# The recurrent half of the output projection as one Strassen step, with weight sums made by adding transfers, and the end of the recurrent branch ahead of the attention

## The chip, the core and the metric

The kernel runs on one core of a Trainium2 chip. The core has five engines that run side by side and wait for one another by semaphores: TensorE (PE; matrix products, with its weight loads shown as PEld), VectorE (DVE), ScalarE (ACT), GpSimd (POOL) and SyncE (SP), which here only issues transfers. Sixteen DMA engines carry the transfers. Weights and activations lie in the on-chip memory SBUF; products arrive in the eight banks of the accumulator memory PSUM, from which VectorE or ScalarE must fetch them.

The metric is the device time of one execution in microseconds, as the median of several runs. A profiled execution gives the trace: when each instruction ran, and what it waited for.

## What is computed

One layer of an encoder: 512 tokens, width 1024, all in float32. The part around the change is this:

```python
y_rnn = (h_f + h_b).astype(x.dtype) * jax.nn.gelu(gate)
...
y_attn = dilated_attention(qh, kh, vh, rel_bias)
mix = jnp.concatenate([rms_norm(y_rnn, norm_rnn_g[l]), rms_norm(y_attn, norm_attn_g[l])], axis=-1)
x = x + mix @ w_out[l]
h = rms_norm(x, mlp_norm_g[l])
x = x + jnp.square(jax.nn.relu(h @ w_up[l])) @ w_down[l]
```

`h_f` and `h_b` are the forward and the backward scan of the recurrent branch (512 channels), `y_attn` comes from eight heads of 64 channels. `w_out` is 1024 x 1024; its upper 512 rows take the recurrent half, its lower 512 rows the attention half. Each half is a product of 512 x 512 by 512 x 1024.

## The kernel before

**Precision.** Each float32 operand is split into a high part, rounded to the fp32r format by a copy, and a low part, the difference. `mm3` (L311) makes a product from three fp32r matmuls: high by high, high by low, low by high. In the text below one *step* is one `mm3`. The high part of a weight block of 128 x 1024 is made by `conv_hi` on ScalarE (L247, tile `whi`), the low part by `conv_lo` on VectorE (L269, tile `wlo`). `remake` makes the low part in another way: two ScalarE copies of 512 columns with the sign turned (L257), onto which two transfers from GpSimd's queue add the raw weights (L259); `conv_lo` then costs VectorE nothing for that block.

**Weights.** All weight blocks form a list `chunks`. `emit_dma` (L226) loads the next plain block into one of three buffers `wraw`, on SP's queue; `conv_lo` calls it when a block's raw weights are done with. The blocks of the recurrent half are the chunks from `C_WO` on, those of the attention half the ones from `C_WA` on. The attention half already goes by one Strassen step, in its form with seven products, in the order `OSEQ`: 11, s2, s3, s4, 21, s1, 22. The sums of its weight blocks are made on VectorE (`sum1` to `sum3` and one more, L1055 to L1066), those of its activations by `o_sum`.

**Order.** PE, ACT, DVE and POOL run strictly in the order in which the Python code issues their instructions. SP does so inside the attention loop as well; outside of it a planner orders SP.

**The attention loop** runs over pairs of heads i = 0 to 4 and steps u = 0 to 3. `att_s` makes the logits of pair i for two u at once (tile `ps`), `att_e` adds the bias and takes the exponential (VectorE and ScalarE, tile `e`), `att_t` turns the exponentials of pair i-1 on TensorE (tile `pt`, fetched by ScalarE as `ett`), `att_c` turns a small strip of them on VectorE, and `att_av` multiplies with the values (tile `pav`, fetched by VectorE as `yp`). `att_z` and `att_zd` send the reciprocal denominators through DRAM. In between, `fill(n)` takes the next n thunks from the list `fillers` and so keeps TensorE busy: first 48 steps of the query and key products for pairs 1 to 3, then the steps of the recurrent half of the output projection. Six are taken ahead of the loop. The table `FILL` says how many of the four places in a step take one; where it says nothing, all four do. The table `plan` holds what else is done in a step: a key (i, u, place). Between the two parts of the list, in (2, 2), stands `load_x`: it places the residual x and four blocks of `w_out` in the buffers that the last query-key product sets free, and spreads the loads over the following steps (`more`, taken by `add_x` at the end of each step).

**The recurrent branch's end.** `rnn_end` adds the two scans and multiplies by the gate (L597, L598), `rnn_sq` squares on ScalarE (L609), `y_add` adds the squares up (L615), `rnn_cols` makes the norm's factor per token, `rc[0]`. These are in `plan`, spread over the loop. `y_hi` and `y_lo` (L621, L625) scale by the norm's weight and split.

**The recurrent half of the projection** is `wo_thunks` (L981): 4 token tiles by 4 channel blocks for each half of the columns, 32 steps in all, each 128 x 128 by 128 x 512. Each of the 8 outputs has a PSUM bank of its own, and `end` multiplies it by `rc[0]` and adds it to x on VectorE:

```python
def end(n, tt):
    stt(x1[tt, n], pw[n, tt], rc[0][:, tt:tt + 1], x1[tt, n], op0=OP.mult, op1=OP.add)
```

By `FILL`, 24 of the 32 steps go into the loop and 8 behind it. Then follows the attention half (`wo_m`, `wo_x`), and the feed-forward part, which takes the rest of the time.

## Time and profile before

| | |
|---|---|
| median of 3 runs | 525.16 us (524.88 to 525.16) |
| the profiled execution's own time | 525.49 us |
| its span, first to last instruction | 523.7 us |
| granted TensorE clock, mean | 0.999 |
| HBM read | 95.59 MB, 191 GB/s over the span |
| steps of the recurrent half on TensorE | 139.6 to 179.6 us, among the attention's |
| `end` on VectorE (L986) | 8 times, 144.6 to 188.7 us |
| loads of x on SP (L1049) | 8 times, 139.9 to 152.6 us |

Times within the trace count from the span's first instruction. Matmuls are pipelined: a row's length (0.39 us for 512 columns) overlaps the next one's, and what counts is the distance from start to start, which the chain of waits gives as a matmul's share (0.23 us). For VectorE and ScalarE, too, the distance between the starts of neighbours that don't wait is what one instruction takes from its engine. A bracket at the end of a row gives the time that the engine stood idle ahead of it and what ended that.

### The profile page before, as it was taken

The numbers are of one execution on the slowest core, as the hardware profiler recorded it, in microseconds if no ns is written. First come the engines' busy times: TensorE is split into PE (matmuls) and PEld (weight loads), VectorE is DVE, ScalarE is ACT, GpSimd is POOL, SyncE is SP. The second block draws the span as 40 slices with busy tenths as digits, with TensorE's granted clock in tenths as the row PEclk, the third lists the DMA queues.
The fourth block names the chain that finished last, engine by engine and source line by source line (L and its number), as shares of the span: only waits on it lengthen the run. The fifth ranks groups of instructions, "written<-read, shape, count | busy, mean of one in ns | idle before, by whom it ended". The sixth has DMA issues, their size and how long they took to land.

```text
span 523.7 us, 8216 instructions
## 1 busy us (share of the span) xinstructions
PE 517.1 (99%) x3021; PEld 444.3 (85%) x3021; DVE 430.4 (82%) x668; ACT 352.2 (67%) x570; POOL 65.3 (12%) x89
## 2 busy tenths in 40 slices
PE   9999999999999999999999999999999999999995
PEld 8867888778777788899999888889999999888884
DVE  6899986788886898898789987789766978986885
ACT  7579946667857857586578666565667577655655
POOL 0173000000000321001300312001100300131000
PEclk9999999999999999999999999999999999999999
DMA  7636555266796499947595899976986497799704
GB/s 288 208 99 196 161 160 180 83 191 199 190 294 197 115 196 247 353 134 195 139 223 143 213 273 281 306 271 161 300 256 168 117 224 210 157 289 257 195 1 161
DMA packets 40329, 105.15 MB, mean 201 GB/s; under 512 B 5056, under 2 KB 13376, under 8 KB 40288
## 3 DMA queue, kind: packets, MB, share of 16 engines
q1 hardware_dynamic: 32448, 78.10, 44.5%
q0 software_dynamic: 7696, 26.32, 27.3%
q8 instruction: 24, 0.39, 0.3%
q10 hardware_dynamic: 144, 0.20, 0.1%
q14 instruction: 17, 0.14, 0.1%
HBM read 95.59 MB, written 4.29 MB: 191 GB/s over the span
## 4 chain that ended last, share of the span: by engine, by line
PE 99%; DVE 0%; issue 0%; DVEq 0%; ACT 0%; ACTq 0%
PE pu L314 10%; PE pu L312 10%; PE pu L313 10%; PE pd L314 10%; PE pd L312 10%; PE pd L313 10%; PE pqk L312 3%; PE pqk L314 3%; PE pqk L313 3%; PE pwo L312 3%; PE pwo L314 3%; PE pwo L313 3%; PE pav L942 2%; PE pt L842 2%; PE ps L806 2%; PE pp L312 1%
## 5 line engine op out<-in xcount | busy, mean ns | idle before, releaser
L269 DVE TENSOR_TENSOR wlo<-wraw,whi 128x1024 fp32r<-128x1024 f32 x71 | 86.6, 1220 | 24.0 <-ACT whi L247 23.9
L247 ACT ACTIVATE whi<-wraw 128x1024 fp32r<-128x1024 f32 x67 | 70.8, 1057 | 37.4 <-PE pd L314 18.4
L313 PE MATMUL pd<-wlo,ah 128*128 128x512 f32 (+1 forms) x195 | 75.2, 386 | 0.0
L312 PE MATMUL pd<-whi,ah 128*128 128x512 f32 (+1 forms) x195 | 75.2, 386 | 0.0
L314 PE MATMUL pd<-whi,al 128*128 128x512 f32 (+1 forms) x195 | 75.2, 386 | 0.0
L313 PE MATMUL pu<-hl,whi 128*128 128x256 f32 x224 | 63.4, 283 | 0.0
L314 PE MATMUL pu<-hh,wlo 128*128 128x256 f32 x224 | 63.4, 283 | 0.0
L312 PE MATMUL pu<-hh,whi 128*128 128x256 f32 x224 | 63.4, 283 | 0.0
L312 PE MATMUL pu<-h2h,whi 128*128 128x256 f32 (+1 forms) x200 | 60.1, 300 | 0.0
L313 PE MATMUL pu<-h2l,whi 128*128 128x256 f32 (+1 forms) x200 | 60.0, 300 | 0.0
L314 PE MATMUL pu<-h2h,wlo 128*128 128x256 f32 (+1 forms) x200 | 60.0, 300 | 0.0
L269 DVE TENSOR_TENSOR wlo<-tw,whi 128x1024 fp32r<-128x1024 f32 x37 | 45.2, 1221 | 17.7 <-ACT whi L247 17.7
L247 ACT ACTIVATE whi<-tw 128x1024 fp32r<-128x1024 f32 x38 | 40.1, 1058 | 24.9 <-PE pd L314 6.3
L312 PEld LDWEIGHTS pu<-hh,whi 128*128 128x128 f32 x224 | 43.0, 192 | 0.0
L313 PEld LDWEIGHTS pu<-hl,whi 128*128 128x128 f32 x224 | 43.0, 192 | 0.0
L314 PEld LDWEIGHTS pu<-hh,wlo 128*128 128x128 f32 x224 | 43.0, 192 | 0.0
L313 PEld LDWEIGHTS pd<-wlo,ah 128*128 128x128 f32 x195 | 36.6, 188 | 7.4
L312 PEld LDWEIGHTS pd<-whi,ah 128*128 128x128 f32 x195 | 36.6, 188 | 7.3
L314 PEld LDWEIGHTS pd<-whi,al 128*128 128x128 f32 x195 | 36.6, 188 | 7.4
L247 ACT ACTIVATE whi<-ts 128x1024 fp32r<-128x1024 f32 x24 | 25.4, 1060 | 25.2 <-PE pd L314 16.4
L313 PEld LDWEIGHTS pu<-h2l,whi 128*128 128x128 f32 x200 | 38.3, 191 | 1.3
L314 PEld LDWEIGHTS pu<-h2h,wlo 128*128 128x128 f32 x200 | 38.3, 191 | 1.3
(280 smaller groups left out, 1220.1 us busy)
## 6 DMA issues: line engine op xcount, KB each, us to landing
wraw<-in_w_up_dram SPq DMA_DIRECT2D x25, 512.0 KB, 4.8
ts<-in_w_dn_dram POOLq DMA_DIRECT2D x24, 512.0 KB, 13.5
wraw<-in_w_dn_dram SPq DMA_DIRECT2D x24, 512.0 KB, 8.7
tw<-in_w_up_dram SPq DMA_DIRECT2D x15, 512.0 KB, 6.7
tw<-in_w_up_dram POOLq DMA_DIRECT2D x15, 512.0 KB, 7.5
wraw<-in_w_in_dram SPq DMA_DIRECT2D x13, 512.0 KB, 4.3
ts<-in_w_dn_dram SPq DMA_DIRECT2D x8, 512.0 KB, 9.0
tw<-in_w_dn_dram SPq DMA_DIRECT2D x8, 512.0 KB, 7.0
```

The lines of the kernel that those rows point to most:

```text
L247: act(hi, raws[i], AF.Copy)
L269: nc.vector.tensor_tensor(lo, r, f(splits[i][0]), op=OP.subtract)
L312: nc.tensor.matmul(o, lhsT=a[0], rhs=b[0], start=bool(first), stop=False, skip_group_check=on)
L313: nc.tensor.matmul(o, lhsT=a[0], rhs=b[1], start=False, stop=False, skip_group_check=on)
L314: nc.tensor.matmul(o, lhsT=a[1], rhs=b[0], start=False, stop=bool(last), skip_group_check=on)
L806: nc.tensor.matmul(psq[p, u][e][:, :NK], lhsT=qs_[p, a][r, P * qt:P * qt + P], rhs=kks[p][r, b, w:w + NK], start=i == 0, stop=i == 2)
L842: nc.tensor.transpose(pt[:, i * P:(i + 1) * P], en[h][qt][:, k:k + P], ident)
L942: nc.tensor.matmul(pav[p][a, co], lhsT=vs[:, jt, h * DH:(h + 1) * DH], rhs=et[h, jt][:, ci], start=jt == 0 and i == 0, stop=jt == 3 and i ...
```

## The change

The recurrent half goes by the same Strassen step as the attention half. `wo_thunks` runs over seven products in the order `RSEQ`: 11, s2, s3, s4, s1, 22, 21, with 2 token tiles and 2 channel blocks each, 28 steps in all. Products 11, s2, s3 and s4 add up in one pair of PSUM banks, s1 and 22 in a second pair, 21 has a third. After each product's token tile, `end` adds the partial sum so far to the quarter of x that `OEND` names; there are 14 of them instead of 8.

- The sums of weight blocks s1, s2 and s3 are loads on SP followed by adding transfers on GpSimd's queue into the same `wraw` buffer; s4 is made by another adding transfer into the buffer of s2, once that one's low part is made. The recurrent half has 7 chunks instead of 4, and `C_WA` and `C_UP` move by 3.
- The sums of activations are made by `strassen_rows`, the attention half's functions turned into a closure that serves both. `rnn_at` scales the branch's output by the norm's weight in place. `rnn_neg` makes the negated factor.
- `rnn_end`, the squares and three of their sums move from the attention loop to the first query-key product and the six steps ahead of the loop; the three sums become adding transfers on GpSimd's queue.
- In `load_x`, the pieces of x come ahead of blocks 22 and 21 and of the sums, which move to later steps; the blocks 21, s2, s3 and s4 of the attention half get their low parts by `remake` within the steps (4, 0) to (4, 2). Before, s4 and 21 did so behind the loop, and s2 and s3 had a `conv_lo`.
- `FILL` takes 20 steps into the loop and leaves 8 behind it.

```diff
+RSEQ = ("11", "s2", "s3", "s4", "s1", "22", "21")
+RSUM = {"s1": ("12", "11"), "s2": ("12", "11", "22"), "s3": ("12", "22")}
...
-    C_G, C_V, C_QK, C_WO, C_WA, C_UP = 4, 8, 12, 20, 24, 31
+    C_G, C_V, C_QK, C_WO, C_WA, C_UP = 4, 8, 12, 20, 27, 34
...
             r = stream.tile([P, 1024], FT, name="wraw", tag="wraw", bufs=3)
-            nc.sync.dma_start(r, source(chunks[i]))
+            c = chunks[i]
+            if isinstance(c, tuple) and c[0] == "r":
+                b = RSUM.get(c[1], (c[1],))
+                nc.sync.dma_start(r, rblock(b[0]))
+                for n in b[1:]:
+                    nc.gpsimd.dma_start(r, rblock(n), accum_op=OP.add)
+            else:
+                nc.sync.dma_start(r, source(c))
             raws[i] = r
...
             if isinstance(c, tuple) and c[0] == "o":
                 return
+            if isinstance(c, tuple) and c[0] == "r":
+                if c[1] == "s2":
+                    nc.gpsimd.dma_start(r, rblock("21"), accum_op=OP.add)
+                    raws[C_WO + RSEQ.index("s4")] = r
+                elif c[1] not in ("22", "21"):
+                    emit_dma()
+                return
...
-        if half in ssy:
+        if half in ssy and half == 0:
+            nc.gpsimd.dma_start(ssy[0], q, accum_op=OP.add)
+        elif half in ssy:
             nc.vector.tensor_tensor(ssy[half], ssy[half], q, op=OP.add)
...
+    o_hi, o_lo, o_hi2, o_lo2, o_sum, o_part = strassen_rows(at)
+    r_hi, r_lo, r_hi2, r_lo2, r_sum, r_part = strassen_rows(yrnn)
+    OEND = {"11": (0, 0), "21": (0, 0), "s1": (1, 1), "22": (0, 1), "s2": (0, 1), "s3": (1, 1), "s4": (1, 0)}
...
-        order = [(0, tt, k) for tt in range(4) for k in range(4)] + [(1, tt, k) for h in (0, 2) for tt in range(4) for k in (h, h + 1)]
+        order = [(w, tt, k) for w in RSEQ for tt in range(2) for k in range(2)]
...
+        def end(j):
+            w, tt, _ = order[2 * j]
+            i, n = OEND[w]
+            g = 2 * i + tt
+            stt(x1[g, n], pw[j], (nrc0 if n else rc[0])[:, g:g + 1], x1[g, n], op0=OP.mult, op1=OP.add)
+
+        def mk(b, w, tt, k):
             def run():
+                j = b // 2
+                new = w in ("11", "s1", "21")
                 if k == 0:
+                    pw[j] = ps_("pwo", "pj") if new else pw[j - 2]
+                hi, lo = splits[C_WO + b // 4]
+                sl = slice(k * S, (k + 1) * S)
+                mm3(pw[j], r_part(w, tt, k), (hi[:, sl], lo[:, sl]), k == 0 and new, k == 1, True)
+                if b % 4 == 1:
+                    conv_hi(C_WO + b // 4 + 3)
+                if b % 4 == 3:
+                    conv_lo(C_WO + b // 4 + 3)
+                if k == 0 and 0 < j < 12:
+                    end(j - 1)
             return run
...
+    RNN = {8: ((rnn_end, 0),), 10: ((rnn_end, 1), (rnn_sq, 0)), 11: ((rnn_end, 2), (rnn_sq, 1)), 13: ((rnn_sq, 2),)}
...
-        more.append([w_in(b22, "22")])
-        more.append([sum1, x_in(2, 0), x_in(3, 0), w_in(b21, "21")])
-        more.append([sum2, x_in(0, 1)])
-        more.append([sum3, x_in(1, 1)])
-        more.append([x_in(2, 1), x_in(3, 1)])
-        more.append([emit_dma])
-        more.append([emit_dma])
-        more.append([emit_dma])
+        more.append([x_in(0, 1), x_in(1, 1)])
+        more.append([w_in(b22, "22"), x_in(2, 1), x_in(3, 1)])
+        more.append([w_in(b21, "21"), x_in(2, 0), x_in(3, 0)])
+        more.append([sum1])
+        more.append([sum2])
+        more.append([sum3, remade_o("21"), remade_o("s2")])
+        more.append([remade_o("s3"), emit_dma])
+        more.append([remade_o("s4"), emit_dma])
...
+    plan = {(0, 0, 0): [op(rnn_at, 2), op(r_sum, "s1", 0)], (0, 0, 2): [op(rnn_at, 1), op(r_sum, "s2", 0)], (0, 0, 3): [op(rnn_at, 3), op(r_sum, "s3", 0)],
+            (0, 1, 1): [op(r_sum, "s1", 1)], (0, 2, 3): [op(r_sum, "22", 0)],
+            (1, 0, 2): [op(r_sum, "s2", 1)], (1, 1, 0): [op(r_sum, "s3", 1)], (1, 1, 2): [op(r_sum, "22", 1)],
+            (1, 3, 2): [op(r_hi, "11", 0), op(r_hi, "11", 1)], (2, 0, 0): [op(r_lo, "11", 0), op(r_lo, "11", 1)], (2, 0, 2): [rnn_cols],
+            (2, 0, 4): [op(r_hi2, "s2")], (2, 1, 2): [rnn_neg], (2, 1, 4): [op(r_lo2, "s2")], (2, 2, 3): [op(r_hi2, "s3")], (2, 3, 1): [op(r_lo2, "s3")],
+            (3, 0, 1): [op(r_hi2, 0)], (3, 0, 3): [op(r_lo2, 0)], (3, 1, 1): [op(r_hi2, 1)], (3, 1, 3): [op(r_lo2, 1)],
+            (3, 2, 1): [op(r_hi2, "s1")], (3, 2, 3): [op(r_lo2, "s1")], (3, 3, 1): [op(r_hi2, "22")], (4, 0, 1): [op(r_lo2, "22")]}
...
+        if n == 2:
+            rnn_end(3)
+            add()
+            rnn_sq(3)
+            rnn_at(0)
+            add()
+        if n == 4:
+            add()
+            add()
         fill(1)
...
-    FILL = {(3, 0): (1, 1, 1, 0), (3, 1): (1, 1, 1, 0), (3, 2): (1, 1, 1, 0), (4, 0): (0, 1, 0, 0), (4, 1): (0, 1, 0, 1), (4, 2): (0, 1, 0, 0), (4, 3): (0, 1, 0, 0)}
+    FILL = {(3, 0): (1, 1, 1, 0), (3, 1): (1, 1, 0, 0), (3, 2): (1, 1, 0, 0), (3, 3): (1, 1, 1, 0), (4, 0): (0, 1, 0, 0), (4, 1): (0, 1, 0, 0), (4, 2): (0, 1, 0, 0), (4, 3): (0, 1, 0, 0)}
...
+    emit_dma()
     fill(1)
-    conv_lo(C_WA + 2)
     att_av(3, range(4))
...
-    remake(C_WA + OSEQ.index("s4"))
     fill(1)
     att_y(3)
     yss = col_sums(ssy[1])
     fill(4)
-    remake(C_WA + OSEQ.index("21"))
+    st["wo"](11)
     fill(len(fillers))
```

The steps, their `end` and their place by `FILL` are then: b0, b1 in (2, 2); b2 to b5 in (2, 3); b6 to b8 in (3, 0); b9, b10 in (3, 1); b11, b12 in (3, 2); b13 to b15 in (3, 3); b16 to b19 in (4, 0) to (4, 3), one each; b20 to b27 behind the loop. `end(j)` belongs to the two steps b = 2j and 2j + 1 and is issued with step 2j + 2. `conv_lo` of the blocks s4, s1, 22, 21 and of the attention half's 11 is issued with steps b3, b7, b11, b15 and b19.

## The prediction

> **What bounds the kernel now.** I read the busy shares first, then the chain of waits.

> ```profile
> PE 517.1 (99%) x3021; PEld 444.3 (85%) x3021; DVE 430.4 (82%) x668; ACT 352.2 (67%) x570; POOL 65.3 (12%) x89
> PE 99%; DVE 0%; issue 0%; DVEq 0%; ACT 0%; ACTq 0%
> ```

> TensorE is busy all the time and the chain runs through it for 99% of the span. So a matmul taken out is worth its pitch, and a hole made in TensorE's work costs its full length: nothing later waits for anybody else and could give it back. What must be asked is whether the other engines still keep ahead where the change adds to their work. The stages of the old projection, by the view of windows (us; busy PE, PEld, DVE, ACT, POOL; granted clock, DMA share):

> ```profile
> 95.00:139.30 44.30, 44.30 (x259) 34.58 (x256) 37.67 (x100) 32.35 (x75) 1.04 (x1) 1.00 0.59 163
> 139.30:159.10 19.80, 19.80 (x115) 16.00 (x115) 15.26 (x42) 14.19 (x39) 0.00 (x0) 1.00 0.92 282
> ```

> From 139 to 159 VectorE has 15.3 of 19.8 us taken, and the DMA engines are at 0.92. The work that the change adds falls mostly there.

> **The change: TensorE.** One step (b of the list `order`) is three matmuls. 32 steps become 28, so 12 matmuls go. The chain (start, length) holds exactly twelve between these two rows:

> ```profile
> 141.77 0.23 PE pwo L312
> ...
> 143.15 0.23 PE pwo L312
> ...
> 144.50 1.33 PE ps L806 x12
> ...
> 159.09 0.66 PE pt L842 x6
> 159.74 5.76 PE pav L942 x48
> 165.50 0.43 PE pwo L312
> ```

> 144.50 - 141.77 = **2.73 us removed**. Three of the four steps go ahead of the `pav` at 159.74, so with full cover it would start at 157.69.

> **A new order between TensorE and VectorE.** Before, each output tile had its own PSUM bank and `end` read it when it liked. Now the products 11, s2, s3 and s4 add up in the same two banks, and `end` reads each partial sum in between: step b4 must wait for `end(0)`, b6 for `end(1)`, up to b14, then b20 and b22. VectorE works in the written order, so everything ahead of an `end` now holds TensorE. VectorE's timeline gives the durations as distances from start to start:

> ```profile
> 140.38 0.74 DVE L625 SCALAR_TENSOR_TENSOR yl<-gt,vt,yh 128x512 fp32r<-128x512 f32 x1
> ...
> 142.28 0.65 DVE L784 TENSOR_TENSOR kk<-kraw,kk 128x512 fp32r<-128x512 f32 x1
> 142.85 1.22 DVE L269 TENSOR_TENSOR wlo<-wraw,whi 128x1024 fp32r<-128x1024 f32 x1
> 144.59 0.75 DVE L986 SCALAR_TENSOR_TENSOR x<-pwo,rcol,x 128x512 f32<-128x512 f32 x1 [0.53 <-DMA x<-in_xn_dram]
> 145.67 0.59 DVE L822 CUSTOM_DVE_ANT_0 e<-ps,tw 128x416 f32<-128x416 f32 x1 [0.33 <-PE ps L806]
> ...
> 146.70 0.30 DVE L851 STREAM_TRANSPOSE ett<-e 128x32 f32<-128x32 f32 x2
> 146.93 0.31 DVE L871 RECIPROCAL rz<-zz 128x32 f32<-128x32 f32 x1
> ...
> 147.41 1.18 DVE L1055 TENSOR_TENSOR ws<-ws,wraw 128x1024 f32<-128x1024 f32 x1
> 148.51 0.58 DVE L822 CUSTOM_DVE_ANT_0 e<-ps,tw 128x416 f32<-128x416 f32 x1
> ...
> 149.75 0.71 DVE L986 SCALAR_TENSOR_TENSOR x<-pwo,rcol,x 128x512 f32<-128x512 f32 x1
> 150.38 1.21 DVE L1059 TENSOR_TENSOR tw<-ws 128x1024 f32<-128x1024 f32 x1
> ...
> 159.11 1.23 DVE L269 TENSOR_TENSOR wlo<-wraw,whi 128x1024 fp32r<-128x1024 f32 x1 [2.16 <-ACT whi L247]
> 160.26 0.74 DVE L986 SCALAR_TENSOR_TENSOR x<-pwo,rcol,x 128x512 f32<-128x512 f32 x1
> ```

> So the softmax part of one attention step (two e and the small transposes) is 1.26, its two e alone 1.03; the reciprocal part 0.48; a sum of 1024 columns 1.10; an `end` 0.63; a low half of 512 columns 0.57 (142.28 to 142.85); one of 1024 columns, `conv_lo`, 1.15.

> VectorE in the new order, by attention step (i, u), from 140.38, where the `yl` that stood there is gone:
> - (2,3): 1.26 + key low half 0.57 + `end(0)` 0.63 + s3 low 0.57 + `conv_lo` 1.15 + `end(1)` 0.63 = 4.81
> - (3,0): 1.26 + 0.48 + 0.63 + 1.15 + 0.63 + 0.57 = 4.72
> - (3,1): 1.26 + 0.63 + 0.57 = 2.46
> - (3,2): 1.26 + 1.15 + 0.63 + 0.57 + sum1 1.10 = 4.71

> That is 16.70 us, and 1.03 more for the two e of (3,3), for whose exponentials the transposes ahead of `pav` wait. TensorE needs less: from 141.11 (the transposes of 0.66 ahead of the first chain row) to 159.09 are 18.0 us for these four steps and (3,3); without the three b steps 15.9, and 13.2 without (3,3) itself (0.66 and three b of 0.68).

> **Waits inside it.** `end(0)` also adds x, which landed only at 144.59 (the bracket above), behind a store that the last query-key matmul sets free. Here it comes up at 142.21: 2.38 us. TensorE reaches b4 at 143.15 (third chain row), so b4 stands 144.59 + 0.75 - 143.15 = 2.2 us: this alone takes four fifths of the gain. How long the other pieces of x take:

> ```profile
> L1049 SPq DMA_DIRECT2D x<-in_xn_dram x8: 424/434/1492, 139.9 to 152.6; - x8
> DMA to landing us min/median/max: 4.1/5.1/5.6
> ```

> Two more pieces now stand on SP's queue behind a weight load whose buffer comes free only with a `conv_lo`. x(0,1) is behind block 21, which waits for the `conv_lo` of s4's weights, done at 146.94: issued at 147.37 (0.43 for the load's own issue), landed at 151.47 at the shortest; `end(2)` comes up at 149.61 (after 0.30 for the logits that the late b4 delays) and waits 1.86. x(2,1) is behind the load after s1's `conv_lo` (153.25) and another: issued at 154.11, landed at 158.21; `end(4)` comes up at 155.71 and waits 2.50. The median landing would add 1.0 to each. In all 2.38 + 0.30 + 1.86 + 2.50 = 7.04, and 140.38 + 17.73 + 7.04 = 165.15 for the second e of (3,3).

> [...]

> ```profile
> 157.41 0.64 ACT L823 ACTIVATE e<-e,mn 128x416 f32<-128x416 f32 x1
> ...
> 166.82 0.87 ACT L845 ACTIVATE ett<-pt 128x384 f32<-128x384 f32 x2 [0.53 <-PE pt L842]
> ```

> One exponential (0.64) and the second head's half of the transposes (0.33) later `pav` starts: 165.15 + 0.97 = 166.1, 8.4 us after 157.69. **Front: 8.4 lost.**

> **Behind `pav`.** VectorE's rows there:

> ```profile
> 165.57 0.69 DVE L948 TENSOR_TENSOR yp<-pav,zrow 128x512 f32<-128x512 f32 x1 [2.14 <-PE pav L942]
> 166.18 0.68 DVE L615 TENSOR_TENSOR ysq<-ysq 128x512 f32<-128x512 f32 x1
> ...
> 168.34 0.42 DVE L919 TENSOR_TENSOR osum<-at 128x256 f32<-128x256 f32 x1 [0.15 <-ACT at L962]
> ...
> 170.15 0.29 DVE L851 STREAM_TRANSPOSE ett<-e 128x32 f32<-128x32 f32 x2
> ```

> After the second y, which waits for both `pav` groups (5.76 + 0.1), stand ahead of `end(8)`: y 0.61, low half 0.57, `end(7)` 0.63, 0.60, sum3 1.10, 0.22, the sums 1.81 (168.34 to 170.15), the sum for s4 1.10, 0.22, and `end(8)` 0.63: 7.5, done 13.4 after the start of `pav`. TensorE wants b20 after 5.76 + 0.90 + 3 x 1.35 = 10.7 (0.90: a step whose first matmul takes 0.43; 1.35: transposes and a step). 2.7 lost, and 0.3 at the third `pav`, whose small transposes come later too. ScalarE has `remake` for four blocks in these steps: four of its 512-column copies, at 0.6 each by the exponential's row, go ahead of the evacuation (`ett`) of (4,1), where 0.53 was spare. That could cost 2.4 - 0.5 = 1.9 more, or nothing, since VectorE holds b20 anyway. I take nothing: VectorE's sum rests on rows of this very place. **Back: 3.0 lost.**

> **Edits that I put at nothing, and their bounds.** The recurrent ends move ahead of the attention:

> ```profile
> 90.28 0.69 DVE L765 TENSOR_TENSOR kraw<-pqk,rrow 128x512 f32<-128x512 f32 x1 [1.36 <-PE pqk L314]
> 96.52 0.69 DVE L597 TENSOR_TENSOR ga<-ga,hs 128x512 f32<-128x512 f32 x1
> ...
> 97.85 0.68 DVE L761 SCALAR_TENSOR_TENSOR qraw<-pqk,rrow 128x512 f32<-128x512 f32 x1
> ```

> Three pairs of 1.33 (96.52 to 97.85) now stand ahead of `kraw`, which waited 1.36 here: at most 2.6 late. Between its product and the first logits TensorE has six steps, 6 x 0.68 = 4.1; `kraw`, ScalarE's copy and the low half take some 2.0 of it (0.69, 0.64 and 0.57 by the rows above). I take nothing; the bounds are 0 and 0.6. Weights by adding transfers:

> ```profile
> 93.88 9.10 SPq L230 DMA_DIRECT2D wraw<-in_w_out_dram  x2
> wraw<-in_w_out_dram SPq DMA_DIRECT2D x5, 512.0 KB, 3.4
> tw<-in_w_up_dram POOLq DMA_DIRECT2D x15, 512.0 KB, 7.5
> 121.47 1.05 ACT L247 ACTIVATE whi<-wraw 128x1024 fp32r<-128x1024 f32 x1
> ```

> s2's weights are one load and two additions; the load is the second of the first row, ended at 102.98 and begun some 0.4 before. 102.6 + 3.4 + 2 x 7.5 = 121.0, needed at 121.47. At a DMA share of 0.59 I take 7.5, so nothing; 3 us more for each would hold ScalarE, and TensorE with it, by up to 5.5. The squares' sums as three adding transfers on POOL end long before they are read. No gain below nothing is left in these: TensorE had no holes to close.

> **The sum.** -2.73 + 8.4 + 3.0 = +8.7 on the profiled execution's 525.49 us (span 523.7); the median of the runs is 0.33 lower, so 525.2 + 8.7 = **533.9 us**, 1.7% slower.

> **Rivals.**
> - *Full cover (faster).* If `end` always comes before its bank is wanted, only 2.73 are left: 522.4. Deciding point: the first `end` done by 143.15; against it stands the bracket at 144.59. Chance 0.10.
> - *Only x's first wait* (no difference): -2.73 + 2.2, 524.6. It needs VectorE to do 16.7 us of work in 13.2: chance 0.12.
> - *VectorE's work, but no waits on SP's queue*: 1.86 and 2.50 fall away: 165.15 - 4.36 = 160.79, `pav` at 161.8, 4.1 lost; -2.73 + 4.1 + 3.0 = +4.4, 529.6. For it: x can land while VectorE is late. Chance 0.25.
> - *The forecast*, 531 to 537: 0.38.
> - *More of the same*: median landings (2.0) and ScalarE's 1.9: 537.8. Chance 0.11.
> - *A falling clock*: holes could lower the granted clock, which is below 1.00 in the last stage alone:

> ```profile
> 441.00:523.70 82.70, 76.86 (x350) 63.88 (x348) 65.92 (x93) 49.76 (x79) 9.65 (x11) 0.99 0.69 183
> ```

> Eight steps at half speed would add 8 x 0.68 = 5.5: 539.4. My longest single hole is 2.5 us. Chance 0.04. [...]

> Within 0.2% (1.05 us) a run can't be told from no change. Faster 0.10, same 0.12, slower 0.78. The range, 524.4 to 538.5, leaves out full cover and the falling clock.

> **What would show it.** Right: TensorE idle at b4, at the second logits of pair 3 and ahead of `pav`, released by VectorE's evacuation; `end(0)`, `end(2)`, `end(4)` waiting for x; VectorE nearly full from 140 to 165; TensorE's busy time 2.7 to 4 us less, the span longer. Wrong: `pwo` at an even pitch with no holes, or x landed ahead of its `end`; or holes at 95 to 125, which would be the weights.

## The result, and the profile after

Median of the runs of the changed kernel: **548.74 us** (546.28 to 549.52), against 525.14 us (524.88 to 525.22) of the kernel before on the same chip: a ratio of 1.0444, 95% interval 1.0423 to 1.0465. The forecast was 533.9 us, with a range up to 538.5. The direction was right; the loss is nearly three times the one forecast and lies outside the range.

The profiled execution took 548.65 us, its span 546.8 us. The page gives busy shares, the clock granted to TensorE by slices (tenths), and the chain of waits:

```profile
PE 521.7 (95%) x3009; PEld 444.4 (81%) x3009; DVE 437.8 (80%) x685; ACT 360.5 (66%) x585; POOL 75.8 (14%) x101
PEclk9999999997979999999999999999999999999999
PE 80%; DVE 7%; DMA 6%; ACT 3%; issue 2%; SPq 0%; DVEq 0%; ACTq 0%
```

TensorE has its 12 instructions less (3009 for 3021), yet is busy 4.6 us longer: from 128.27 to 135.10 and from 152.17 to 159.00 us its granted clock was 0.50 (the windows below), and there matmuls of 512 columns started 0.43 us apart (131.74 to 134.73) instead of 0.23. The chain, which ran through TensorE alone before, now goes through VectorE, the DMA and ScalarE for 16% of the span. The timeline of TensorE, longer idle stretches (start, length, tile, idle time before and what ended it):

```profile
128.76 0.48 PE L864 MATMUL pt<-ident,e 128*128 128x128 f32 x1 [2.32 <-ACT ett L867]
129.76 1.33 PE L864 MATMUL pt<-ident,e 128*128 128x128 f32 x5 [0.53 <-ACT e L845]
...
145.48 0.40 PE L337 MATMUL pwo<-whi,oh 128*128 128x512 f32 x1
...
154.88 0.79 PE L337 MATMUL pwo<-whi,oh 128*128 128x512 f32 x1 [5.83 <-DVE x L1021]
...
169.94 0.50 PE L337 MATMUL pwo<-whi,oh 128*128 128x512 f32 x1 [1.76 <-DVE x L1021]
...
173.54 0.50 PE L337 MATMUL pwo<-whi,oh 128*128 128x512 f32 x1 [1.27 <-DVE x L1021]
...
176.55 1.06 PE L864 MATMUL pt<-ident,e 128*128 128x128 f32 x5 [1.25 <-ACT e L845]
177.55 5.83 PE L974 MATMUL pav<-ett,vs 128*64 128x416 f32 x48
...
187.03 0.93 PE L864 MATMUL pt<-ident,e 128*128 128x128 f32 x6 [1.40 <-ACT ett L867]
...
190.38 0.93 PE L864 MATMUL pt<-ident,e 128*128 128x128 f32 x6 [1.73 <-ACT ett L867]
```

Three rows divide the loss into the terms of the forecast: the first step of the projection (145.48), the value products of pairs 1 and 2 (177.55), and the first matmul of the feedforward (`pu`), which closes the stretch. The starts of these three in every kernel of this study, and the distances between them:

| kernel | median us | ratio to before [95%] | first step at | to `pav` | to `pu` |
|---|---|---|---|---|---|
| before | 525.14 | | 139.57 | 20.10 | 40.83 |
| changed, if nothing waited | | | 139.57 | 18.05 | 40.15 |
| changed | 548.74 | 1.0444 [1.0423, 1.0465] | 145.48 | 32.07 | 45.72 |
| e1_plain_s2 | 540.68 | 1.0299 [1.0280, 1.0317] | 140.32 | 30.49 | 45.75 |
| e2_x_first | 540.36 | 1.0287 [1.0268, 1.0305] | 145.82 | 22.95 | 45.75 |
| e3_early_end | 525.38 | 1.0003 [0.9993, 1.0012] | 139.56 | 20.11 | 40.82 |
| e4_remake_late | 549.57 | 1.0473 [1.0454, 1.0492] | 144.22 | 31.09 | 47.90 |
| e5_both | 534.29 | 1.0178 [1.0158, 1.0198] | 139.77 | 22.72 | 45.76 |
| e6_own_bank | 534.95 | 1.0187 [1.0170, 1.0203] | 140.52 | 24.08 | 45.77 |
| e7_early_s2 | 534.92 | 1.0198 [1.0171, 1.0226] | 140.23 | 23.24 | 45.76 |
| e8_early_splits | 535.61 | 1.0195 [1.0168, 1.0223] | 139.38 | 22.87 | 45.87 |
| e9_no_x | 534.51 | 1.0180 [1.0163, 1.0197] | 139.38 | 23.61 | 45.77 |
| e10_no_remake | 533.44 | 1.0157 [1.0140, 1.0174] | 140.40 | 22.73 | 43.94 |
| e11_sums_pool | 536.65 | 1.0214 [1.0187, 1.0240] | 140.44 | 22.46 | 49.25 |
| e13_splits_no_x | 532.00 | 1.0120 [1.0095, 1.0145] | 140.67 | 20.02 | 45.76 |
| e14_no_pool | 530.19 | 1.0094 [1.0075, 1.0113] | 140.29 | 20.33 | 43.79 |
| e12_all | 527.42 | 1.0043 [1.0028, 1.0058] | 140.04 | 19.23 | 42.86 |

The starts and distances are those of the one profiled execution of each kernel. The runs were made on several chips: the kernel before has a median of 525.38 us beside e1 to e4, 525.20 beside e5 to e8, 524.70 beside e9 to e12 and 525.67 beside e13 and e14, so medians of different groups can't be compared to better than about 1 us. One of the four runs of e14_no_pool was slow (1322.85 us) and is left out.

The second row is the one before less the matmuls removed: nine of the twelve lie ahead of `pav`, and 9 x 0.2275 = 2.05, 3 x 0.2275 = 0.68. Against it the changed kernel loses 145.48 - 139.57 = **5.9** ahead of the projection, 32.07 - 18.05 = **14.0** in front of `pav` and 45.72 - 40.15 = **5.6** behind it. Less 2.73 that is 22.8 of the 23.1 us by which the span grew. The forecast had 0, 8.4 and 3.0.

**The 5.9 ahead of the projection.** First SP's and GpSimd's issues of the recurrent weights, then the adding transfers' median time to landing from 88 to 130 (last figure), then ScalarE's copy of s2's weights:

```profile
95.88 8.63 SPq L244 DMA_DIRECT2D wraw<-in_w_out_dram  x2
```

```profile
108.17 0.86 POOL L246 DMA_DIRECT2D wraw<-in_w_out_dram  x1 [8.20 <-DMA tw<-nbd]
117.28 1.75 POOL L246 DMA_DIRECT2D wraw<-in_w_out_dram  x2 [8.25 <-DMA tw<-nbd]
```

```profile
wraw<-in_w_out_dram POOLq DMA_DIRECT2D x5, 512.0 KB, 9.9
```

```profile
127.27 1.06 ACT L265 ACTIVATE whi<-wraw 128x1024 fp32r<-128x1024 f32 x1 [5.57 <-DMA wraw<-in_w_out_dram]
128.24 0.85 ACT L867 ACTIVATE ett<-pt 128x384 f32<-128x384 f32 x2
```

s2's load is the second of the first row. The second addition waits for the first: issued at 108.17 and 117.28 (the other issue in that row is s3's), 9.1 apart, the second landed about 127.2. (The brackets name `tw<-nbd`, another transfer; in e7_early_s2 below the trace puts the same wait down to `wraw` itself.) So the copy of the weights, due at 121.47 before, came at 127.27, and in ScalarE's written order the softmax's evacuation `ett` stood behind it. That makes the holes of 2.32 and 0.53 us. The clock fell in the first of them, at 128.27. Windows of TensorE's timeline (stretch, length, busy PE and the other engines, then the granted clock, third from the end):

```profile
124.86:128.27 3.41, 1.58 (x14) 1.06 (x12) 0.00 (x0) 1.00 (x2) 0.00 (x0) 1.00 1.06 224
...
128.27:131.69 3.42, 2.40 (x8) 1.86 (x9) 1.75 (x3) 3.42 (x12) 0.86 (x1) 0.50 1.05 243
131.69:135.10 3.41, 3.41 (x9) 2.64 (x8) 1.68 (x8) 1.36 (x5) 0.00 (x0) 0.50 1.11 298
135.10:138.52 3.42, 3.42 (x19) 2.87 (x18) 3.18 (x11) 2.57 (x5) 0.01 (x1) 1.00 0.80 183
```

For 6.83 us the granted clock was 0.50; TensorE was busy 2.40 + 3.41 = 5.81 of it. Taken as half the work, that is an estimated 2.9 lost; by the two distances of 0.43 and 0.23 it is 2.7. 2.32 + 0.53 + 2.9 = 5.75, nearly all of the 5.9.

There was an earlier wait in this stage, on VectorE. Its first sum of activations waited 2.50 us for ScalarE, which scales the branch's output there (`rnn_at`), and a low half of weights stood behind that sum:

```profile
99.37 0.42 DVE L945 TENSOR_TENSOR osum<-gt 128x256 f32<-128x256 f32 x1 [2.50 <-ACT gt L1049]
...
102.94 1.22 DVE L287 TENSOR_TENSOR wlo<-wraw,whi 128x1024 fp32r<-128x1024 f32 x1
```

SP issued s2's load as that low half ended, at 104.2 where the kernel before has 102.6. It also cost TensorE something: the logits at 101.62 waited 0.43 for VectorE. The two traces don't run level up to here (VectorE's `qraw` starts at 84.84 before, at 84.13 here). Counted from that row, the stage loses 6.6, and the 0.9 beyond the 5.75 stands in e7_early_s2 too (140.23 - 84.64 = 55.59 against 139.57 - 84.84 = 54.73), but not in e3_early_end, which has no such sums.

**The 14.0 in front of `pav`.** SP's and VectorE's rows:

```profile
141.46 0.33 SPq L244 DMA_DIRECT2D wraw<-in_w_out_dram  x1
...
145.44 0.33 SPq L1096 DMA_DIRECT2D ws<-in_w_out_dram  x1
145.88 1.30 SPq L1093 DMA_DIRECT2D x<-in_xn_dram  x2
```

```profile
154.08 0.75 DVE L1021 SCALAR_TENSOR_TENSOR x<-pwo,rcol,x 128x512 f32<-128x512 f32 x1 [5.90 <-DMA x<-in_xn_dram]
...
169.13 0.75 DVE L1021 SCALAR_TENSOR_TENSOR x<-pwo,nrc,x 128x512 f32<-128x512 f32 x1 [3.50 <-DMA x<-in_xn_dram]
```

x(0,0) was issued at 145.88 behind two loads of 512 KB (141.46 and 145.44) and landed 8.2 us later; `end(0)` stood 5.90 us at the head of VectorE's queue and b4 5.83 us behind it. The clock was at 0.50 again, from 152.17 to 159.00:

```profile
148.76:152.17 3.41, 0.30 (x2) 0.00 (x0) 0.00 (x0) 2.69 (x7) 0.00 (x0) 1.00 0.99 329
...
152.17:155.58 3.41, 0.69 (x2) 0.60 (x3) 1.50 (x3) 0.00 (x0) 0.00 (x0) 0.50 0.19 64
155.58:159.00 3.42, 3.42 (x14) 2.42 (x14) 1.64 (x2) 0.00 (x0) 0.00 (x0) 0.50 0.37 110
159.00:162.40 3.40, 3.24 (x21) 2.31 (x18) 2.80 (x10) 2.17 (x7) 0.00 (x0) 1.00 0.96 280
```

0.69 + 3.42 = 4.11 busy at a clock of 0.50: 2.06 lost by the same estimate of half the work. b4's hole is 3.6 longer than the 2.2 forecast; 3.6 + 2.06 = 5.7 is as much as the difference between 14.0 and 8.4. That it fits so well is partly luck, since other waits of the forecast moved both ways: `end(2)` didn't wait for x (forecast 1.86), `end(4)` waited 3.50 (forecast 2.50).

**The 5.6 behind `pav`.** ScalarE's timeline ahead of the first late `ett`: the table load, four 512-column copies of `remake`, then the evacuation for which TensorE waits 1.40 us.

```profile
183.03 1.28 ACT L1200 ACT_TABLE_LOAD   x1
...
184.43 1.13 ACT L275 ACTIVATE wlo<-ws 128x512 fp32r<-128x512 f32 x2
185.47 1.13 ACT L275 ACTIVATE wlo<-tw 128x512 fp32r<-128x512 f32 x2
186.51 0.85 ACT L867 ACTIVATE ett<-pt 128x384 f32<-128x384 f32 x2
```

### The profile page after: what moved, and what is told of

It is laid out like the page before. It is cut to its first block, busy times and chain, and to the rows that moved or that the text cites. A ratio compares the mean times of both kernels' runs of the same rounds, so it can differ in the third digit from the quotient of the medians.

```text
span 546.8 us, 8272 instructions
## 1 busy us (share of the span) xinstructions
PE 521.7 (95%) x3009; PEld 444.4 (81%) x3009; DVE 437.8 (80%) x685; ACT 360.5 (66%) x585; POOL 75.8 (14%) x101
## 4 chain that ended last, share of the span: by engine, by line
PE 80%; DVE 7%; DMA 6%; ACT 3%; issue 2%; SPq 0%; DVEq 0%; ACTq 0%
PE pu L337 10%; PE pu L338 10%; PE pu L339 10%; PE pd L337 9%; PE pd L338 9%; PE pd L339 9%; DMA wraw<-in_w_out_dram 2%; PE pav L974 2%; PE pp L337 1%; PE pp L338 1%; PE pp L339 1%; PE pv L339 1%; PE pv L337 1%; PE pv L338 1%; DMA kk<-kk 1%
## 5 line engine op out<-in xcount | busy, mean ns | idle before, releaser
L287 DVE TENSOR_TENSOR wlo<-wraw,whi 128x1024 fp32r<-128x1024 f32 x74 | 90.1, 1218 | 24.5 <-ACT whi L265 24.2
L265 ACT ACTIVATE whi<-wraw 128x1024 fp32r<-128x1024 f32 x70 | 73.9, 1056 | 43.2 <-PE pd L339 18.2
L287 DVE TENSOR_TENSOR wlo<-tw,whi 128x1024 fp32r<-128x1024 f32 x36 | 44.0, 1222 | 19.8 <-ACT whi L265 19.8
L337 PEld LDWEIGHTS pu<-h2h,whi 128*128 128x128 f32 x200 | 38.3, 191 | 1.3
## 6 DMA issues: line engine op xcount, KB each, us to landing
wraw<-in_w_up_dram SPq DMA_DIRECT2D x25, 512.0 KB, 4.8
ts<-in_w_dn_dram POOLq DMA_DIRECT2D x24, 512.0 KB, 13.0
wraw<-in_w_dn_dram SPq DMA_DIRECT2D x24, 512.0 KB, 8.4
tw<-in_w_up_dram SPq DMA_DIRECT2D x15, 512.0 KB, 6.1
tw<-in_w_up_dram POOLq DMA_DIRECT2D x15, 512.0 KB, 8.5
wraw<-in_w_in_dram SPq DMA_DIRECT2D x13, 512.0 KB, 3.4
ts<-in_w_dn_dram SPq DMA_DIRECT2D x8, 512.0 KB, 7.4
tw<-in_w_dn_dram SPq DMA_DIRECT2D x8, 512.0 KB, 8.9
```

Of the source, the lines that this page charges most:

```text
L265: act(hi, raws[i], AF.Copy)
L287: nc.vector.tensor_tensor(lo, r, f(splits[i][0]), op=OP.subtract)
L337: nc.tensor.matmul(o, lhsT=a[0], rhs=b[0], start=bool(first), stop=False, skip_group_check=on)
```

## The experiments

### Late weights and x's place on the queue

Run e1_plain_s2:

```diff
-RSUM = {"s1": ("12", "11"), "s2": ("12", "11", "22"), "s3": ("12", "22")}
+RSUM = {"s1": ("12", "11"), "s2": ("12",), "s3": ("12", "22")}
```

> Leaves out the two adding transfers of s2's weights (block 12 alone is loaded), so the weights of s2 and s4 are not the sums. Theory: the late weights of s2 (5.57 us of ScalarE's wait, TensorE holes of 2.3 and 0.5 us behind it, and some 6 us at half clock) cost 4 to 8 us: 540 to 545 us, ScalarE's copy of s2's weights back at about 121.5, no hole before 138. Rival, that VectorE's work holds the evacuations from 145 on anyway: 547 or more, since TensorE then only waits longer there.

540.68 us, 8.1 less than the changed kernel. The copy of s2's weights is back in its place, without a wait, and TensorE has no hole from 103 to 140:

```profile
122.22 1.04 ACT L265 ACTIVATE whi<-wraw 128x1024 fp32r<-128x1024 f32 x1
```

The first step comes at 140.32 instead of 145.48. So the weights were nearly the whole of the first term; what is left is the wait at the activation sums, which this kernel still has.

Run e2_x_first: the loads of the recurrent blocks 22 and 21 and of the attention's blocks 11 and 12 go behind the first pieces of x.

```diff
-                elif c[1] not in ("22", "21"):
+                elif c[1] == "11":
...
-        w_in(b12, "12")()
         x_in(0, 0)()
-        more.append([x_in(1, 0)])
+        x_in(1, 0)()
         more.append([x_in(0, 1), x_in(1, 1)])
-        more.append([w_in(b22, "22"), x_in(2, 1), x_in(3, 1)])
-        more.append([w_in(b21, "21"), x_in(2, 0), x_in(3, 0)])
-        more.append([sum1])
+        more.append([emit_dma, w_in(b12, "12")])
+        more.append([x_in(2, 1), x_in(3, 1), emit_dma])
+        more.append([x_in(2, 0), x_in(3, 0), emit_dma, w_in(b22, "22")])
+        more.append([w_in(b21, "21"), sum1])
```

> The whole computation; SP issues x's pieces ahead of the loads of blocks 22 and 21 and of the first attention block, which are taken out of the low halves and put behind them. Theory (x(0,0), issued behind a load that waited for a low half, landed at 154.1 and held b4 for 5.8 us, x(2,1) held end(4) for 3.5): b4's hole falls to 3 us or less, 540 to 544 us. Rival, that VectorE's work from 145 to 178 sets pav's start whatever x does: the waits for x go, pav moves by 2 us at most, 546 or more.

540.36 us. x's first pieces are issued no earlier than before, and yet `end(0)` starts at 148.93, with no wait:

```profile
146.02 1.76 SPq L1093 DMA_DIRECT2D x<-in_xn_dram  x4
```

```profile
148.93 0.75 DVE L1021 SCALAR_TENSOR_TENSOR x<-pwo,rcol,x 128x512 f32<-128x512 f32 x1
```

So it was not the time of issue but the megabyte issued ahead of it: x landed in 2.9 us at most instead of 8.2. From the first step to `pav` 22.95 us instead of 32.07. The rival (VectorE sets `pav`'s start whatever x does) fell.

Run e5_both has both edits.

> Both edits of the first two runs together: s2's weights as one plain load (s2's and s4's weights are then not the sums) and x's pieces issued first. Theory: two separate losses of about 8 us each, so they add: 531 to 534 us, no hole before 145, and what is left above before is VectorE's work and ScalarE's evacuations behind pav. Rival, that they hide the same loss (TensorE late by the one is what the other waits for): 537 or more.

534.29 us. The two gains of 8.06 and 8.38 add but for 2.0 (548.74 - 534.29 = 14.45), so they are two losses, and the rival (one loss that both hide) fell. In no stage from 88 to 201 was the granted clock under 1.00.

Run e7_early_s2 keeps the whole computation: e2_x_first, and s2's load changes places with block 11's.

```diff
     plain = deque(i for i, c in enumerate(chunks) if in_order(c))
+    at20 = plain.index(C_WO)
+    plain[at20], plain[at20 + 1] = C_WO + 1, C_WO
```

> The whole computation; x's pieces first as before in this study, and s2's load ahead of block 11's, so that its two adding transfers start some 4 to 8 us earlier. Theory (the transfers are late by about as much as they start late): within 2 us of the run with both edits, 531 to 536 us, no hole at 128. Rival, that the adding transfers or the DMA queues are too slow however early they start: 538 or more, with ScalarE's copy of s2's weights still behind 125.

534.92 us. The additions are issued at 101.06 and 106.68 instead of 108.17 and 117.28, and ScalarE's copy of s2's weights waits for nothing. Started 7 us earlier, the additions are in time, the first of them in 5.6 us instead of 9.1. These two reorderings, which leave no work out, give back 13.8 of the 23.6 us.

### The ends ahead of the attention

Run e3_early_end is the kernel before with `rnn_end`, `rnn_sq` and the squares' adding transfers where the change has them, and no Strassen step:

```diff
-        if half in ssy:
+        if half in ssy and half == 0:
+            nc.gpsimd.dma_start(ssy[0], q, accum_op=OP.add)
+        elif half in ssy:
...
+    RNN = {8: ((rnn_end, 0),), 10: ((rnn_end, 1), (rnn_sq, 0)), 11: ((rnn_end, 2), (rnn_sq, 1)), 13: ((rnn_sq, 2),)}
...
+        for fn, t in RNN.get(n, ()):
+            fn(t)
...
+        if n == 2:
+            rnn_end(3)
+            add()
+            rnn_sq(3)
+            add()
```

> The kernel before, with only the recurrent ends moved ahead of the attention and the squares' sums made by adding transfers; no Strassen step. Theory: they cost nothing and, since VectorE's steps of the attention are then lighter, bring nothing either: 524.6 to 525.6 us. Rival, that their 4 us on VectorE at 90 to 98 and POOL's transfers are part of the loss: 526.5 or more, with holes in TensorE between 88 and 125.

525.38 us beside 525.38 for the kernel before: nothing, within 0.1%. The row sums of the change aren't in this kernel. TensorE has no hole from 88 to 139.3:

```profile
88.00:139.30 51.30, 51.30 (x291) 40.21 (x290) 38.83 (x100) 36.11 (x79) 3.70 (x4) 1.00 0.65 174
```

### Is it the shared buffer, VectorE's work, or x?

Run e6_own_bank stands on e5_both.

```diff
-                new = w in ("11", "s1", "21")
+                new = True
```

> As the run with both edits, and every block's sum gets a PSUM buffer of its own, so that no product waits for the evacuation of the product before it in a shared buffer; what a product would have added to the sum before it is left out. Theory: the holes at pwo are waits for a shared buffer that VectorE is late to read, and VectorE has more work there than TensorE leaves time for, so the holes move to the softmax's buffers and the time falls by 0 to 2 us. Rival, that the sharing itself (one step between an evacuation and the next use) is the loss: 3 us or more below the run with both edits.

534.95 us, no change. TensorE still waits for VectorE's evacuations, now twice ahead of `pav`, where e5_both has one such wait of over 0.3 us, 1.29 at 158.49:

```profile
156.75 0.50 PE L337 MATMUL pwo<-whi,oh 128*128 128x512 f32 x1 [1.53 <-DVE x L1021]
...
160.35 0.50 PE L337 MATMUL pwo<-whi,oh 128*128 128x512 f32 x1 [1.29 <-DVE x L1021]
```

A buffer of its own for each product doesn't help here, since the evacuations as such come late.

Runs e8_early_splits and e9_no_x each change e7_early_s2 in one thing: the splits of four blocks of rows move ahead, or x is left out.

```diff
-            (3, 0, 1): [op(r_hi2, 0)], (3, 0, 3): [op(r_lo2, 0)], (3, 1, 1): [op(r_hi2, 1)], (3, 1, 3): [op(r_lo2, 1)],
-            (3, 2, 1): [op(r_hi2, "s1")], (3, 2, 3): [op(r_lo2, "s1")], (3, 3, 1): [op(r_hi2, "22")], (4, 0, 1): [op(r_lo2, "22")]}
+            (0, 1, 3): [op(r_hi2, 0)], (0, 2, 1): [op(r_lo2, 0)], (0, 3, 1): [op(r_hi2, 1)], (0, 3, 3): [op(r_lo2, 1)],
+            (1, 0, 1): [op(r_hi2, "s1")], (1, 0, 3): [op(r_lo2, "s1")], (1, 2, 1): [op(r_hi2, "22")], (1, 2, 3): [op(r_lo2, "22")]}
```

> The whole computation; the run before, and the splits of rows 0, 1, s1 and 22 (four copies on ScalarE, four subtractions on VectorE of 0.6 us each) are moved from the stretch of 142 to 165 back to that of 100 to 135. Theory: VectorE's work inside 140 to 178 is what is left of the front's loss, 2.3 us of it go: 1.5 to 3.5 us below the run before. Rival, that what is left lies in the softmax's waits and behind pav: within 1 us of the run before.

```diff
-            stt(x1[g, n], pw[j], (nrc0 if n else rc[0])[:, g:g + 1], x1[g, n], op0=OP.mult, op1=OP.add)
+            stt(x1[g, n], pw[j], (nrc0 if n else rc[0])[:, g:g + 1], x1[g, n] if (g, n) in seen else ssy[0], op0=OP.mult, op1=OP.add)
+            seen.add((g, n))
...
-            return lambda: nc.sync.dma_start(x1[g, n], xn[2 * g + n])
+            return lambda: None
```

> As the run with s2's load first, and x left out: its eight transfers are not issued, and the first evacuation into each piece adds the row of squares in place of x, with the same instruction. Theory now (what is left of the front's loss is VectorE's in-order queue held at its head by x's landings, 1.1 and 1.8 us): 2 to 4 us below the run with s2's load first, no hole at b4. Rival (VectorE's sheer work in 140 to 163): within 1 us of it.

535.61 and 534.51 us: neither moved anything beyond 1 us, both theories missed. Once the splits are gone, VectorE waits for x in their place (e8_early_splits, VectorE's timeline):

```profile
143.32 0.75 DVE L1023 SCALAR_TENSOR_TENSOR x<-pwo,rcol,x 128x512 f32<-128x512 f32 x1 [1.13 <-DMA x<-in_xn_dram]
...
154.19 0.75 DVE L1023 SCALAR_TENSOR_TENSOR x<-pwo,nrc,x 128x512 f32<-128x512 f32 x1 [1.78 <-DMA x<-in_xn_dram]
```

Without x the splits stand there instead. If each covers the other, both edits together must give what neither gives alone. Run e13_splits_no_x has both:

> As the run with s2's load first, with both edits that alone changed nothing: the splits moved early and x left out. Theory (VectorE's work and x's landings cover each other): 2 to 4 us below that run, 531 to 533 us, with the value products of pairs 1 and 2 starting 2 to 4 us earlier. Rival (what helped in the run with everything was the sums on GpSimd or the copies left out): within 1 us of it, 534 or more.

532.00 us (530.46 to 532.50, where e7_early_s2 had 534.32 to 537.07): 2.9 less, and from the first step to `pav` 20.02 instead of 23.24. The wait ahead of the last transposes is 0.37 instead of 1.22:

```profile
159.69 1.06 PE L866 MATMUL pt<-ident,e 128*128 128x128 f32 x5 [0.37 <-ACT e L847]
```

### Behind the value products

Run e4_remake_late, on the changed kernel:

```diff
-        more.append([sum3, remade_o("21"), remade_o("s2")])
-        more.append([remade_o("s3"), emit_dma])
-        more.append([remade_o("s4"), emit_dma])
+        more.append([sum3])
+        more.append([emit_dma])
+        more.append([emit_dma])
...
+    remake(C_WA + OSEQ.index("s4"))
...
+    remake(C_WA + OSEQ.index("21"))
```

> The whole computation; the low halves of the attention blocks s2 and s3 go back to VectorE and those of s4 and 21 back behind the loop, as in the kernel before, so that ScalarE has four remakes less inside pair 4. Theory (ScalarE's remakes ahead of the evacuations ett make the holes of 1.40 and 1.73 us behind pav): 1 to 3 us less than the changed kernel, 545.5 to 547.5. Rival, that VectorE holds pair 4: no change or slower, 548 to 551, with the holes named for VectorE instead.

549.57 us, no gain. The hole ahead of `ett` shrinks, others grow, at VectorE's evacuation and then at ScalarE's splits of the attention's rows. Behind the last of them the clock was at 0.50 from 204.64 to 208.06, with TensorE busy all the time: by the estimate of half the work, 1.7 of the 2.2 us by which the last stretch is longer. TensorE's rows:

```profile
185.27 0.93 PE L864 MATMUL pt<-ident,e 128*128 128x128 f32 x6 [0.52 <-ACT ett L867]
188.92 0.50 PE L337 MATMUL pwo<-whi,oh 128*128 128x512 f32 x1 [2.02 <-DVE x L1021]
...
203.30 0.47 PE L337 MATMUL pwo<-whi,oh 128*128 128x512 f32 x1 [2.76 <-ACT oh L923]
```

This moves work from one engine to the other and can't price it. Run e10_no_remake, on e7_early_s2, leaves it out:

```diff
+            if isinstance(c, tuple) and c[0] == "o" and c[1] in ("21", "s2", "s3", "s4"):
+                splits[i] += (splits[i][0],)
+                return
...
-        return lambda: remake(C_WA + OSEQ.index(n))
+        return lambda: None
```

> As the run with s2's load first, and the low halves of the attention blocks 21, s2, s3 and s4 are left out (their first halves stand in), so ScalarE has eight 512-column copies less and nothing takes their place on VectorE. Theory (the copies ahead of the evacuations ett make the holes of 1.4 and 1.7 us behind pav): 2 to 3.5 us below that run. Rival (VectorE's sums and evacuations hold the last product there anyway): within 1 us of it, the holes named for VectorE.

533.44 us: 1.5 less, short of the 2 to 3.5 expected, and only 1.0 less where each is set against the kernel before on its own chip (8.7 above it, e7_early_s2 9.7). The median alone doesn't decide against the rival; the trace does, where the last stretch falls from 45.76 to 43.94. The wait of 1.41 at the first `ett` is gone, and the one for VectorE's evacuation behind it grows from 0.87 to 2.04. Run e14_no_pool makes the same edit on e13_splits_no_x:

> As the run before this one, and the low halves of the attention blocks 21, s2, s3 and s4 are left out too; the four sums stay on VectorE. Theory (ScalarE's copies cost behind the value products what VectorE's work doesn't cover): 1.5 to 3 us below the run before this one, 528.5 to 531 us. Rival (the sums on VectorE hold the place): within 1 us of the run before this one.

530.19 us, 1.8 less on the same chip, the stretch 43.79. So ScalarE's copies cost 1.8 to 2.0 us there.

Run e11_sums_pool, on e7_early_s2:

```diff
-        tt = nc.vector.tensor_tensor
+        tt = nc.gpsimd.tensor_tensor
```

> The whole computation; as the run with s2's load first, and the four sums of the attention's weight blocks (1.14 us each) go from VectorE to GpSimd. Theory (VectorE waits at such a sum for block 11's load and the softmax waits behind it): 1 to 3 us below that run. Rival (the copies of the low halves wait for the sums, which GpSimd makes more slowly): no gain, or up to 3 us slower.

536.65 us: nothing gained. The last stretch is 3.5 longer in the profiled execution (537.54 us), but there the clock was at 0.50 from 174.1 to 184.3, with TensorE busy for 8.0 us: by the estimate of half the work 4.0 lost, more than the 3.5. The mean clock of the other three runs (0.996 and 0.997, where this one has 0.987) shows no such fall, so the stretch doesn't price the sums. GpSimd's sums take twice VectorE's 1.22 us and more, and VectorE's low half beside them, otherwise 1.18, takes 2.89 (GpSimd's timeline, then VectorE's):

```profile
160.25 2.57 POOL L1101 TENSOR_TENSOR ws<-ws,wraw 128x1024 f32<-128x1024 f32 x1 [24.26 <-DMA wraw<-in_w_out_dram]
162.90 2.37 POOL L1105 TENSOR_TENSOR tw<-ws 128x1024 f32<-128x1024 f32 x1
```

```profile
158.13 1.18 DVE L289 TENSOR_TENSOR wlo<-wraw,whi 128x1024 fp32r<-128x1024 f32 x1
...
163.46 2.89 DVE L289 TENSOR_TENSOR wlo<-wraw,whi 128x1024 fp32r<-128x1024 f32 x1 [1.02 <-ACT whi L267]
```

Run e12_all puts all of it together: e14_no_pool with the sums on GpSimd.

> All of it at once: splits moved early, x left out, the four low halves left out, the four sums on GpSimd. Theory, that the loss left in the run with s2's load first is the sum of these waits: 524 to 529 us. Rival, that a part sits elsewhere (the chain from logits to transposes has fewer steps beside it): 530 or more.

527.42 us, with x and four low halves left out: still 1.0043 of before (interval to 1.0058). Of the losses, 0.5, 1.2 and 2.7 us are left in the three stretches, more than the 2.73 removed. Against e14_no_pool, which differs by the sums alone, the two last stretches are 1.1 and 0.9 shorter: the sums on GpSimd gain 2.0 us here, where x and the copies made from them are gone, and gained nothing in e11_sums_pool.

## Why the prediction came out wrong

- *Removed work, 2.73*: the 12 matmuls are gone; no run shows their time alone, since every one still had holes.
- *Recurrent ends and squares' sums, put at nothing*: right, 525.38 beside 525.38. The row sums that took the ends' place in the loop aren't in the forecast at all; they cost the 0.9 above.
- *s2's weights, put at nothing*: **the first step that failed**. "102.6 + 3.4 + 2 x 7.5 = 121.0, needed at 121.47" left half a microsecond of slack, and took the 7.5 from other adding transfers because the DMA share of the stage was 0.59; with the change's own transfers in it, it was 0.96 and 0.92 while the two additions ran. It was also the shortest of the medians at hand: the page before has 24 adding transfers of 512 KB (`ts`) with 13.5. The first addition was issued 2.2 later than the sum had it (108.17 for 106.0): 1.6 by the load, which came behind the row sums, and 0.6 by its landing. The two additions took 9.1 and some 9.9. ScalarE waited 5.57, where the bound named was 5.5. Its consequence for the clock wasn't in the bound at all.
- *x(0,0), 2.2 at b4*: **mis-sized**, 5.83. The mechanism is the one forecast, but the landing was taken over from the kernel before (4.1 to 5.6 after the issue), though the new order puts the loads of the recurrent block 22 and of the attention's block 12 ahead of it; it took 8.2, and 2.9 at most with those loads behind it (e2_x_first). The 531 at the lower end of the forecast's band was the author's estimate; the shortest landing of x before, from which 533.9 was worked out, was 4.1.
- *x(0,1) and x(2,1) on SP's queue, 1.86 and 2.50*: the order was right (`end(4)` waited 3.50); `end(2)` didn't wait, since it came up late itself, at 161.30, behind a wait of 2.34 for logits from a TensorE whose clock was 0.50 up to 159.00.
- *Falling clock, 0.04*: **the rival that was thrown out came true**, besides the forecast and not in its stead. "My longest single hole is 2.5 us" was the argument against it; that so short a hole leaves the clock alone was the author's estimate, not shown by any trace, and the first fall, at 128.27, came within a hole of 2.32. An estimated 2.9 + 2.06 = 5.0 us were lost, beside the 5.5 worked out; that the two are so close is luck, since the 5.5 was for eight steps of the projection at half speed, and the first fall met query-key products.
- *VectorE's work*: with the late transfers out of the way (e7_early_s2), front 23.24 - 18.05 = 5.2 lost. The forecast without SP's waits had 4.1. That the ledger of VectorE and the landings of x add up, as the forecast did, is shown false for what is left: each hides the other, and only both together (e13_splits_no_x) give 3.2 back.
- *Back, 3.0*: **mis-sized**, 5.6. ScalarE's copies were put at "1.9 more, or nothing, since VectorE holds b20 anyway", and nothing was taken. They cost 1.8 to 2.0 (e10_no_remake, e14_no_pool): the holes come one after the other, 1.40 and 1.73 at `ett` before `end` is asked for at all. The remaining 0.6 to 0.8 has no run of its own.

Together 5.9 + 5.6 + 2.6 = 14.1 us of 14.4 by which the changed kernel's span grew beyond the forecast's 8.7. That the time came out longer, as forecast, is no luck: TensorE did wait for VectorE's evacuations and for x, by the mechanism of the forecast, but the terms put at nothing made up more than half of what was missed. It stays open whether an order exists in which the step pays: the best whole computation tried here took 534.92 us, and no run beat the kernel before.

## What to carry to other kernels

In a kernel whose matrix engine has no holes, an edit "put at nothing" has a bound on one side only, and several of them fail together: take the unfavourable end of each as a case of its own. Take a transfer's time from its new place on the queue, with the megabytes then ahead of it (here 8.2 us against 2.9 at most), not from the old place. Two causes that each hold the same queue can't be priced by removing one; remove both.

## What the runs showed of the hardware

```profile
128.64:132.05 3.41, 1.58 (x8) 1.11 (x9) 1.27 (x2) 3.41 (x10) 0.86 (x1) 1.00 1.10 228
132.05:135.47 3.42, 3.42 (x9) 2.67 (x8) 1.01 (x3) 1.34 (x4) 0.00 (x0) 0.50 1.01 292
```

```profile
159.70:163.13 3.43, 1.35 (x9) 0.87 (x7) 0.73 (x2) 1.68 (x4) 0.00 (x0) 1.00 0.97 348
163.13:166.56 3.43, 3.36 (x11) 2.88 (x12) 3.43 (x10) 2.21 (x7) 0.00 (x0) 0.50 0.65 226
```

A stretch busy 1.63 us, with the hole of 1.40 us behind `pav` in it, was followed by one at 1.00 (the changed kernel):

```profile
186.30:189.71 3.41, 1.63 (x9) 1.08 (x9) 1.78 (x5) 3.41 (x7) 2.63 (x3) 1.00 0.97 293
189.71:193.12 3.41, 1.88 (x10) 1.33 (x11) 3.41 (x10) 2.73 (x8) 1.94 (x3) 1.00 1.02 295
```

The longest single holes ahead of these three falls, the second of the changed kernel (5.83) apart, were 2.32, 2.29 and 2.16 us. From 88 to 215 us of the five traces with falls (the changed kernel, e1, e2, e4, e11), the busiest stretch at 1.00 that was followed by one at 0.50 had 1.58 us, and the least busy one that was followed by one at 1.00 had 1.62 (e1_plain_s2, 180.21 to 183.62). Of the stretches at 0.50, the ones busy 0.69 and 2.40 us (the changed kernel, 152.17 and 128.27) and 2.65 (e11_sums_pool, 177.51) were followed by another at 0.50, those busy 3.36 (e1_plain_s2, 163.13) and 3.41 or 3.42 (the changed kernel, e2_x_first) by one at 1.00.
